# Delta rule on a hybrid diffusion step: triangular solves in blocks of 16 instead of 32, a convolution that accumulates in PSUM, and transfers issued on GpSimd and ACT

## The chip, the cores and the metric

One core of a Trainium2 chip runs the whole program. The metric is the device time of one execution in microseconds, taken over several executions; a separate profiled execution gives the trace. The core's engines are called by their names in the profile: PE is TensorE (matrix products, with PEld for its weight loads), DVE is VectorE, ACT is ScalarE, POOL is GpSimd and SP is SyncE, which here does nothing but issue transfers. Each engine takes its instructions in order, from a list that is fixed when the program is built.

## The reference, cut to what matters

The program is one step of a two-layer model over 640 tokens (128 of a prompt and 512 of a sample) of width 1024. Layer 0 mixes tokens with a state-space scan and attention, layer 1 with a gated delta rule; each layer ends in a two-matrix MLP with a hidden width of 4096. The change lies mostly in the delta rule of layer 1, which the reference computes as follows (for both directions of time, 8 heads of 128 channels, chunks of 64 tokens there):

```python
proj = h @ w_in
qkv = silu(dwconv(proj[..., :3 * D_MODEL], conv_w))       # 5 taps along the tokens
g = -exp(a_log) * softplus(a_in + dt_bias)                # log decay, per head
beta = sigmoid(b_in)
q, k = l2norm(q) * DN_DK ** -0.5, l2norm(k)
# in _gdn_chunked, per chunk
decay  = exp(where(tri_incl, gcum[..., :, None] - gcum[..., None, :], -inf))
a_mat  = where(tri_strict, (kb @ k.T) * decay, 0.0)       # the Gram block
t_mat  = triangular_solve(eye + a_mat, eye)               # the solve
u_c, w_c = t_mat @ (v * beta), t_mat @ (kb * exp(gcum))
# a scan over chunks with the state s
v_new = u_i - w_i @ s
o     = (q_i * exp(g_i)) @ s + at_i @ v_new
s     = s * exp(g_last) + (k_i * exp(g_last - g_i)).T @ v_new
# after the scan
out = (rmsnorm(o_f + o_b) * silu(z)) @ w_out
```

## The kernel before, in words

The kernel keeps the 640 tokens along the free dimension and channels on the partitions. A list planner of the framework orders the instructions of every engine when the program is built: each instruction has a priority from its place in the program, a block under `high_priority(offset=n)` counts as if it stood n instructions earlier, and a buffer (a tile with a tag and a number of `bufs`) is handed on when its last reader is done. PSUM is divided into four tags of two banks each, `pg`, `pa`, `pb` and `pc`.

**Matrix products of projections and MLPs.** `gemm` walks over blocks of 128 output channels. `weight` loads one block of weights (512 KB, tile `raw`, two buffers) with a transfer issued on SP, ACT rounds it to a high part `whi` (L194) and POOL subtracts to get the low part `wlo` (L196). `mm_step` then makes three products per 128 input channels, in two halves of 320 tokens: L205, L206 and L207, 48 matrix products for a block. This routine serves 153 weight blocks of the whole program.

**Layer 1** (the method `odd`) works on four pairs of heads, `pr` 0 to 3. `gdn_project` makes the pair's six blocks of k, q and v (`m` 0 to 5). Its `ev` evacuates each block to the SBUF tile `cb` with padding columns, and runs the convolution there: an ACT multiplication for tap 0 (L1319), four DVE multiply-adds over 642 columns (L1322), an ACT tanh, and a last DVE multiply-add in two pieces (L1335, L1336). For some blocks the last tap or the last product is made by ACT and POOL instead (L1325 and L1326; L1331 to L1333). Squares, transposes to token order and normalization follow, with banks of tag `pc`.

**Gram blocks.** `gdn_group` is called once for each of five chunks of 128 tokens, out of `mid`. It makes the decay matrix (POOL L1376, ACT L1379), the Gram product in a `pb` bank (PE L1395), the products with decay (DVE L1400) and beta (POOL L1401), and writes the result to DRAM (`udg`, `utd`), from where the 32x32 diagonal blocks return to the tile `ub`, one block in each of 80 partitions.

**The solve.** `gdn_blocks` inverts these 32x32 triangles by elimination: 31 steps of two DVE instructions each, a product into `sbt` (L1425) and a subtraction from `ub` (L1427), on 31 to 256 elements. `gdn_inverse` then builds the 128x128 inverses: ten POOL products with a mask and ten DVE transposes for a pair (twice: L1453, L1454), and 140 small matrix products in `pb` banks (L1458), first to 64x64 and then to 128x128.

**The chain.** `gdn_chain` runs the scan over the chunks: `prep` loads what a step needs (`cka`, `ckb`, `cbc`, `cgq`), multiplies q by its decay on POOL (four products, L1567) and makes the attention block (PE L1570); then come PE L1615, L1625, L1631, L1632 and L1643 with DVE L1620 and L1646 between them. Chains 0 to 2 use banks `pa`, the last one `pb`.

**Order.** `solve` calls what is left of the pair's `blocks` generator (that is `gdn_blocks`), then `gdn_inverse` and `gdn_chain` at an offset of 10000. In the program it stands behind the projection of the next pair. For the last pair, the eight blocks of the gate z (`zproj`, evacuation L1721 to L1724) are put in, too. Behind all that stand filling products of the modulation (L282), the gating, and the output projection in two halves (`odd` and `odd_out`, residual in L423).

Transfers: all of them are issued on SP, one after the other.

## Time and profile before

| what | value |
|---|---|
| time, median of 3 runs | 1972.41 us (1968.0 to 1977.28) |
| time of the profiled execution | 1975.42 us |
| its span, first to last instruction | 1973.2 us |
| mean granted TensorE clock | 0.965 |
| PE busy | 1798.4 us (91%) |
| DVE busy | 1279.3 us (65%) |
| ACT busy | 875.5 us (44%) |
| POOL busy | 760.1 us (39%) |
| transfers | 286.60 MB, 45.4% of 16 engines' time on the SP queue |

The profile lists, for the profiled execution, when each instruction ran, on which engine and for how long, which instruction ended an engine's wait, and which clock TensorE was granted. A matrix product of 32-bit operands that are not rounded appears in it as two records. "Busy" of a group is the time in which at least one of its instructions ran.

### The profile page before, as it was taken

What the parts mean: (1) busy time and instruction counts of PE and PEld (TensorE: products, weight loads), DVE (VectorE), ACT (ScalarE), POOL (GpSimd) and SP (SyncE); (2) the same over time, 40 slices, a digit from 0 to 9 for tenths busy, and PEclk for the clock granted to TensorE, in tenths of its full rate; (3) what the DMA queues carried; (4) which work ended last, traced back from release to release, by engine and by line L of the source; (5) the groups of instructions that cost most, each with busy time, mean ns of one, the idle gap of its engine ahead of it and who ended that gap; (6) DMA issues with size and microseconds to landing.
All of it is one profiled execution on the core that took longest, in us unless ns stands there. A gap on an engine that the chain in (4) does not pass through costs nothing. (4 is left out here: it accounts for less than half of the span.)

```text
span 1973.2 us, 35750 instructions
## 1 busy us (share of the span) xinstructions
PE 1798.4 (91%) x13556; PEld 1696.1 (86%) x13556; DVE 1279.3 (65%) x2797; ACT 875.5 (44%) x1956; POOL 760.1 (39%) x609
## 2 busy tenths in 40 slices
PE   5789799989999999997878888798989899999998
PEld 3789677978999999997877888787878799999997
DVE  8998777269273644547589988674667927364553
ACT  4344466344243443535454455344324425344362
POOL 2522101541343343453455555522245334343451
PEclk9989899999999999998998999999999999999999
DMA  8446886533332222332576468758844122222221
GB/s 319 131 122 167 248 264 205 201 121 126 109 117 76 77 85 82 135 117 72 163 208 197 117 196 239 222 166 269 274 137 149 54 97 76 86 76 86 76 97 54
DMA packets 206983, 286.60 MB, mean 145 GB/s; under 512 B 54878, under 2 KB 138236, under 8 KB 206812
## 3 DMA queue, kind: packets, MB, share of 16 engines
q1 hardware_dynamic: 206812, 284.33, 45.4%
q8 instruction: 107, 1.75, 0.4%
q14 instruction: 64, 0.52, 0.1%
HBM read 228.87 MB, written 46.82 MB: 140 GB/s over the span
## 5 line engine op out<-in xcount | busy, mean ns | idle before, releaser
L196 POOL TENSOR_TENSOR wlo<-raw,whi 128x1024 fp32r<-128x1024 f32 (+1 forms) x153 | 359.3, 2351 | 509.1 <-ACT whi L194 462.3
L194 ACT ACTIVATE whi<-raw 128x1024 fp32r<-128x1024 f32 (+1 forms) x153 | 153.1, 1001 | 329.1 <-PE pg L206 146.8
L207 PE MATMUL pg<-hidh,wlo 128*128 128x320 f32 (+2 forms) x576 | 178.8, 311 | 0.6 <-POOL wlo L196 0.6
L205 PE MATMUL pg<-hidh,whi 128*128 128x320 f32 (+2 forms) x576 | 179.0, 311 | 0.0
L206 PE MATMUL pg<-hidl,whi 128*128 128x320 f32 (+2 forms) x576 | 178.9, 311 | 0.0
L423 DVE SCALAR_TENSOR_TENSOR x<-pg,mod,x 128x128 f32<-128x128 f32 (+2 forms) x132 | 53.7, 436 | 182.2 <-PE pg L207 182.2
L205 PE MATMUL pg<-h10h,whi 128*128 128x320 f32 x472 | 158.4, 336 | 14.7 <-DVE cb L1722 7.0
L207 PE MATMUL pg<-h10h,wlo 128*128 128x320 f32 x472 | 155.4, 329 | 1.7 <-POOL wlo L196 1.7
L206 PE MATMUL pg<-h10l,whi 128*128 128x320 f32 x472 | 155.7, 330 | 0.0
L205 PE MATMUL pa<-hidh,whi 128*128 128x320 f32 x448 | 138.0, 310 | 1.1 <-ACT whi L194 1.1
L207 PE MATMUL pa<-hidh,wlo 128*128 128x320 f32 x448 | 138.4, 309 | 0.0
L206 PE MATMUL pa<-hidl,whi 128*128 128x320 f32 x448 | 138.2, 309 | 0.0
L423 DVE SCALAR_TENSOR_TENSOR x<-pa,mod,x 128x128 f32<-128x128 f32 (+2 forms) x108 | 43.9, 435 | 133.1 <-PE pa L207 133.1
L508 POOL TENSOR_TENSOR wq<-S,wq 128x512 fp32r<-128x512 f32 x52 | 71.3, 1371 | 115.3 <-ACT wq L507 115.3
L205 PEld LDWEIGHTS pg<-h10h,whi 128*128 128x128 f32 x472 | 95.8, 203 | 18.3 <-DVE cb L1722 8.0
L207 PEld LDWEIGHTS pg<-hidh,wlo 128*128 128x128 f32 x576 | 108.2, 188 | 1.6 <-POOL wlo L196 1.1
L205 PEld LDWEIGHTS pg<-hidh,whi 128*128 128x128 f32 x576 | 108.3, 188 | 0.9 <-issue 0.8
L206 PEld LDWEIGHTS pg<-hidl,whi 128*128 128x128 f32 x576 | 108.2, 188 | 0.4 <-DVE hidl L569 0.3
L1322 DVE SCALAR_TENSOR_TENSOR cv<-cb,cw,cv 128x642 f32<-128x642 f32 x90 | 95.8, 1065 | 10.4 <-ACT cv L1319 9.2
L207 PEld LDWEIGHTS pg<-h10h,wlo 128*128 128x128 f32 x472 | 95.4, 202 | 2.1 <-POOL wlo L196 1.9
L206 PEld LDWEIGHTS pg<-h10l,whi 128*128 128x128 f32 x472 | 95.7, 203 | 0.6 <-issue 0.4
L205 PEld LDWEIGHTS pa<-hidh,whi 128*128 128x128 f32 x448 | 83.9, 188 | 2.7 <-ACT whi L194 1.8
(743 smaller groups left out, 5745.4 us busy)
## 6 DMA issues: line engine op xcount, KB each, us to landing
raw<-in_wff SPq DMA_DIRECT2D x104, 512.0 KB
mraw<-in_wmod SPq DMA_DIRECT2D x96, 512.0 KB
raw<-in_wino SPq DMA_DIRECT2D x33, 512.0 KB
rawx<-in_wff SPq DMA_DIRECT2D x24, 512.0 KB
raw<-in_wine SPq DMA_DIRECT2D x16, 512.0 KB
cka<-pd SPq DMA_DIRECT2D x28, 256.0 KB
ckb<-pd SPq DMA_DIRECT2D x28, 256.0 KB
s5g<-s5g SPq DMA_DIRECT2D x32, 164.0 KB
```

The lines of the kernel that those rows point to most:

```text
L194: nc.scalar.activation(hi[:, :kt], raw[:, :kt], AF.Copy)
L196: (nc.vector if self.lov and self.nw % self.lov else nc.gpsimd).tensor_tensor(lo[:, :kt], raw[:, :kt], hi[:, :kt], op=ALU.subtract)
L205: nc.tensor.matmul(p[:, :n], hi[:, k], xh[:, s], start=(k == 0), stop=False)
L206: nc.tensor.matmul(p[:, :n], hi[:, k], xl[:, s], start=False, stop=False)
L207: nc.tensor.matmul(p[:, :n], lo[:, k], xh[:, s], start=False, stop=(k == kt - 1))
L423: nc.vector.scalar_tensor_tensor(x[m][:, s], p[:, ls], g, x[m][:, s], op0=ALU.mult, op1=ALU.add)
L508: (V if j % 2 else nc.gpsimd).tensor_tensor(t[:, 4:8], src, t[:, 0:4], op=SU)
L1322: V.scalar_tensor_tensor(cv, cb[m][:, t:t + 642], cw[:, t:t + 1], cv, op0=M, op1=AD)
```

## The change

1. `gdn_blocks` inverts 16x16 triangles: the two halves of each 32x32 block at once, 15 steps of two DVE instructions on 30 to 128 elements, into a tile of its own (`ubd`, set to zero by POOL). `ub` has one buffer instead of two.
2. `gdn_inverse` gets a first stage that joins 16x16 inverses into 32x32 ones: 160 matrix products of 32x32x32 for a pair, two ACT copies, two DVE subtractions. The mask products on POOL and most transposes go; ACT copies place the blocks. The other 140 products now name a row of the array as well as a column. Its loads from DRAM go from 3 to 14 transfers, issued on SP.
3. The convolution (`conv`) works on the prompt's 128 columns in SBUF and on the sample's 512 columns in a PSUM bank of tag `pc`, all taps and the last product on DVE, for all 24 blocks.
4. Gram products use `pc` banks instead of `pb`. `solve` is called when `m == 1` of the next pair's projection has been evacuated, in front of that pair's Gram blocks; `gdn_blocks` is called at the end of its own pair's projection.
5. Issue of transfers: all weight loads of `weight` and the store `udg` move from SP to GpSimd, the stores `ed` and `zod` to ACT.
6. The product of q with its decay moves from POOL (four instructions of 128 columns) to DVE (two of 256). The evacuation of z uses another buffer.

```diff
@@ weight
-        nc.sync.dma_start(out=raw[:, :kt], in_=src)
+        nc.gpsimd.dma_start(out=raw[:, :kt], in_=src)
@@ gdn_project
+        def conv(x, cw):
+            cv = self.tl([128, 642], "cv")
+            cl = self.ps("pc")
+            parts = ((cv[:, 0:128], 0), (cl, 130))
+            for o, c0 in parts:
+                nc.scalar.activation(o, x[:, c0:c0 + o.shape[1]], AF.Identity, scale=cw[:, 0:1])
+            for t in range(1, 5):
+                for o, c0 in parts[::-1]:
+                    V.scalar_tensor_tensor(o, x[:, c0 + t:c0 + t + o.shape[1]], cw[:, t:t + 1], o, op0=M, op1=AD)
+            for o, c0 in parts[::-1]:
+                nc.scalar.activation(x[:, c0:c0 + o.shape[1]], o, AF.Tanh)
+            for (o, c0), c1 in zip(parts[::-1], (128, 0)):
+                V.scalar_tensor_tensor(cv[:, c1:c1 + o.shape[1]], x[:, c0:c0 + o.shape[1]], 1.0, o, op0=AD, op1=M)
+            return cv
@@ gdn_group
-        nc.sync.dma_start(out=ed[:, c], in_=E)
-        pk = self.ps("pb")
+        nc.scalar.dma_start(out=ed[:, c], in_=E)
+        pk = self.ps("pc")
...
-            nc.sync.dma_start(out=self.ap(ud, o + 10 * d * self.US, [[128, 128], [self.US, 2], [1, 128]]),
+            nc.gpsimd.dma_start(out=self.ap(ud, o + 10 * d * self.US, [[128, 128], [self.US, 2], [1, 128]]),
@@ gdn_blocks
-        D = ub
-        V.memset(D.rearrange("p a b -> p (a b)")[:, 0:1024:33], 1.0)
-        for j in range(31):
-            n, m = 31 - j, j + 1
...
+        D = P.tile([80, 32, 32], F32, name="ubd", bufs=1)
+        nc.gpsimd.memset(D, 0.0)
+        nc.gpsimd.memset(D.rearrange("p a b -> p (a b)")[:, 0:1024:33], 1.0)
+        for j in range(15):
+            n, m = 15 - j, j + 1
+            sh = [80, 2, n, m]
...
+            V.tensor_tensor(t, both(ub, j, 1, j + 1, n).rearrange("p s a b -> p s b a").to_broadcast(sh),
+                            both(D, j, 1, 0, m).to_broadcast(sh), op=ALU.mult)
+            V.tensor_tensor(both(D, j + 1, n, 0, m), both(D, j + 1, n, 0, m), t, op=ALU.subtract)
@@ gdn_inverse
-        cm = P.tile([128, 20, 32], F32, name="gcm")
-        nc.sync.dma_start(out=cm, in_=self.ap(dd, 0, [[32, 128], [4096, 20], [1, 32]]))
+        Dc, Tc, Gc, Xc = (P.tile([128, 2, 10, 32], F32, name=n) for n in ("gDc", "gTc", "gGc", "gXc"))
+        for d, t in ((0, Dc), (1, Tc)):
+            for hh in range(2):
+                nc.sync.dma_start(out=t[:, d, hh::2], in_=...)
+        G.memset(Gc, 0.0)
+        for d in range(2):
+            for k in range(4):
+                nc.sync.dma_start(out=Gc[r:r + 16, d, :, j:j + 16], in_=...)
-        for c in range(5):
-            for d, a, b in ((0, D, TT), (1, TT, D)):
-                G.tensor_tensor(a[...], src, mask, op=ALU.mult)
-                V.transpose(two(b, c, d), two(a, c, d))
+        V.transpose(fl(Tc[:, 0]), fl(Dc[:, 0]))
+        V.transpose(fl(Dc[:, 1]), fl(Tc[:, 1]))
+        px = [bank() for d in range(2)]
+        for d in range(2):
+            for n in range(10):
+                for r in S:
+                    mm(px[d][r, n], Gc[r, d, n], Dc[r, d, n], r.start, r.start)
+            ACT.activation(Xc[:, d], px[d], AF.Copy)
+        px = [bank() for d in range(2)]
+        for d in range(2):
+            for n in range(10):
+                for r in S:
+                    mm(px[d][r, n], Tc[r, d, n], Xc[r, d, n], r.start, r.start)
+            V.tensor_tensor(Dc[:, d], Dc[:, d], px[d], op=ALU.subtract)
+            V.transpose(fl(Tc[:, d]), fl(Dc[:, d]))
+        G.memset(D64, 0.0)
+        G.memset(TT, 0.0)
...
@@ gdn_chain, prep
-                for u in range(4):
-                    nc.gpsimd.tensor_tensor(gq[:, u], gq[:, u], lds[u][2 + u % 2], op=M)
+                for d in range(2):
+                    V.tensor_tensor(gq[:, 2 * d:2 * d + 2], gq[:, 2 * d:2 * d + 2], lds[2 * d][8], op=M)
@@ odd
-            th = self.tl([128, HB], "cb")
+            th = self.sp.tile([128, HB], F32, name="zth", tag="acc", bufs=2)
...
-            nc.sync.dma_start(out=zds[m][:, s], in_=th)
+            nc.scalar.dma_start(out=zds[m][:, s], in_=th)
...
             def mid(m, pd):
+                if m == 1 and held:
+                    solve(*held)
...
+                if m == 5:
+                    got.append(next(steps[0]))
             pd = self.gdn_project(pr, hn, P, first if pr == 0 else None, mid)
-            if held:
-                solve(*held)
-            held = pr, pd, steps[0]
+            held = pr, pd, got[0]
```

## Rows read from the trace of the kernel before

**Rows 1.** The page's list of engines: busy us, share of the span, instructions.
```profile
PE 1798.4 (91%) x13556; PEld 1696.1 (86%) x13556; DVE 1279.3 (65%) x2797; ACT 875.5 (44%) x1956; POOL 760.1 (39%) x609
```
**Rows 2.** Stretches: length, busy PE, PEld, DVE, ACT, POOL, granted clock, transfers.
```profile
600.00:700.00 100.00, 100.00 (x684) 100.00 (x684) 48.39 (x90) 39.49 (x76) 40.20 (x23) 1.00 0.25 80
880.00:1020.00 140.00, 119.28 (x784) 114.47 (x783) 99.34 (x187) 78.33 (x171) 63.08 (x78) 0.91 0.49 143
1020.00:1160.00 140.00, 114.00 (x964) 109.94 (x963) 136.86 (x263) 70.12 (x149) 80.67 (x75) 0.89 0.54 158
1160.00:1330.00 170.00, 148.56 (x1499) 139.08 (x1498) 131.36 (x352) 81.90 (x195) 82.60 (x89) 0.96 0.74 211
1330.00:1465.00 135.00, 122.29 (x1173) 106.86 (x1171) 68.51 (x214) 47.86 (x112) 34.52 (x50) 0.97 0.73 239
```
**Rows 3.** A stretch of L1425 alone: DVE busy, mostly the elimination of pair 0.
```profile
1020.00:1100.00 80.00, 18.20 (x34) 0.89 0.56 168
```
**Rows 4.** Stretches of L1458 alone (PE, PEld): the inverse of pair 0.
```profile
990.00:1100.00 110.00, 0.00 (x0) 0.00 (x0) 0.89 0.64 186
1100.00:1140.00 40.00, 6.21 (x280) 5.13 (x280) 0.91 0.44 121
```
**Rows 5.** Layer 1 as one stretch: DVE time of L1425, L1427, L1322, in this order.
```profile
880.00:1465.00 585.00, 64.70 (x124) 0.94 0.63 189
880.00:1465.00 585.00, 72.58 (x124) 0.94 0.63 189
880.00:1465.00 585.00, 95.76 (x90) 0.94 0.63 189
```
**Rows 6.** DVE's timeline: start us, us, instruction; then POOL's.
```profile
1030.31 0.27 DVE L1427 TENSOR_TENSOR ub<-ub,sbt 80x112 f32<-80x112 f32 x1
1030.61 0.29 DVE L1425 TENSOR_TENSOR sbt<-ub 80x135 f32<-80x135 f32 x1
...
1052.23 2.49 DVE L1427 TENSOR_TENSOR ub<-ub,sbt 80x252 f32<-80x252 f32 x1
...
1051.88 2.57 POOL L196 TENSOR_TENSOR wlo<-raw,whi 128x1024 fp32r<-128x1024 f32 x1
```
**Rows 7.** Single lines of DVE: shortest, median and longest in ns.
```profile
L1400 DVE TENSOR_TENSOR gau<-pb,gbg x20: 674/678/692, 972.2 to 1253.0; 128x512 f32<-128x512 f32 x20
L1322 DVE SCALAR_TENSOR_TENSOR cv<-cb,cw,cv x90: 758/878/3014, 909.6 to 1246.8; 128x642 f32<-128x642 f32 x90
L1335 DVE SCALAR_TENSOR_TENSOR cv<-cb,cv x16: 277/280/427, 922.6 to 1256.6; 128x128 f32<-128x128 f32 x16
```
**Rows 8.** POOL by line and shape, 840 to 1500: busy us, mean ns.
```profile
L1567 POOL TENSOR_TENSOR cgq<-cgq,cka 128x128 f32<-128x128 f32 x64 | 31.8, 524 | 84.6 <-DVE cgl L1565 45.4 <-DMA cka<-pd 22.5 <-DVE ogn_t L180 7.7
...
L1453 POOL TENSOR_TENSOR gTT<-gcm,cst 128x256 f32<-128x256 f32 x20 | 18.6, 932 | 0.0
...
L1453 POOL TENSOR_TENSOR gD<-gcm,cst 128x256 f32<-128x256 f32 x20 | 16.2, 811 | 11.8 <-DMA gcm<-dd 11.8
L1333 POOL TENSOR_TENSOR cv<-cb,cv 128x512 f32<-128x512 f32 x8 | 12.0, 1502 | 0.0
L1326 POOL TENSOR_TENSOR cv<-cv,cb 128x642 f32<-128x642 f32 x6 | 9.9, 1646 | 5.9 <-ACT cb L1325 5.9
```
**Rows 9.** PE by line and shape, 840 to 1500: small products of the inverse.
```profile
L1458 PE MATMUL pb<-gD,guf 128*32 128x32 f32 x320 | 8.3, 210 | 10.9 <-DVE gD L1454 6.7 <-DVE osm L1663 3.7 <-POOL gD L1453 0.3
...
L1458 PE MATMUL pb<-gTT,gcm 128*32 128x32 f32 x320 | 4.8, 199 | 0.0
```
**Rows 10.** SP's own waits, 880 to 1470: us in total, times, longest.
```profile
SPq L193 <- POOL wlo L196: 46.0, 13, 7.3
SPq L1724 <- ACT cb L1723: 26.0, 6, 11.4
```
**Rows 11.** SP issuing weight loads (shortest, median, longest ns).
```profile
L193 SPq DMA_DIRECT2D raw<-in_wino x33: 327/376/1099, 855.5 to 1293.6; - x33
```
**Rows 12.** The page's groups: POOL's share of preparing all weight blocks.
```profile
L196 POOL TENSOR_TENSOR wlo<-raw,whi 128x1024 fp32r<-128x1024 f32 (+1 forms) x153 | 359.3, 2351 | 509.1 <-ACT whi L194 462.3
```

More of the change, by code (lines that the diff above doesn't have):

```diff
@@ L1455, in gdn_inverse @@
-        CH = [(c, hh) for c in range(5) for hh in range(2)]
-        def mm(out, l, r, col):
-            nc.tensor.matmul(out, l, r, start=True, stop=True, tile_position=(0, col))
-        def bank(n):
-            return self.ps("pb")[:, :320].rearrange("p (c h j) -> p c h j", c=5, h=2)
-        p = bank(0)
-        for c, hh in CH:
+        D64 = P.tile([128, 10, 64], F32, name="gD64")
+        fl = lambda t: t.rearrange("p n j -> p (n j)")
+        V.transpose(fl(Tc[:, 0]), fl(Dc[:, 0]))
+        V.transpose(fl(Dc[:, 1]), fl(Tc[:, 1]))
@@ new lines, in mm, with bank @@
+        def mm(out, l, r, row, col):
+            nc.tensor.matmul(out, l, r, start=True, stop=True, tile_position=(row, col))
+        def bank():
+            return self.ps("pb")[:, :320].rearrange("p (n j) -> p n j", n=10)
+        S = [slice(32 * k, 32 * k + 32) for k in range(4)]
+        px = [bank() for d in range(2)]
[4 more added lines that the diff above has]
+            ACT.activation(Xc[:, d], px[d], AF.Copy)
@@ L1466, in gdn_inverse @@
+        for d in range(2):
+            for r in S:
+                ACT.activation(TT[r, :, u2(d), r], ch(Tc[r, d]), AF.Copy)
+            for k in range(2):
+                r = S[2 * d + k]
+                ACT.activation(D64[r, :, 32 * k:32 * k + 32], Dc[r, d], AF.Copy)
+        p = bank()
+        for n in range(10):
+            c, hh = divmod(n, 2)
             for a in (0, 64):
                 x, y = slice(a, a + 32), slice(a + 32, a + 64)
-                mm(p[y, c, hh], uo[:, 0, c, hh, a:a + 32], D[:, c, hh, x], a + 32)
@@ L1476, in gdn_inverse @@
-        ACT.activation(D[32:64, :, 0:2, 0:32], pD[32:64], AF.Copy, scale=-1.0)
-        ACT.activation(D[64:96, :, 2:4, 96:128], pD[64:96], AF.Copy, scale=-1.0)
-        for c, hh in CH:
+        pD, pT = bank(), bank()
+        for n in range(10):
+            mm(pD[32:64, n], Tc[32:64, 0, n], X[32:64, n], 32, 32)
+            mm(pD[64:96, n], Tc[64:96, 1, n], X[64:96, n], 64, 64)
+        ACT.activation(D64[32:64, :, 0:32], pD[32:64], AF.Copy, scale=-1.0)
+        ACT.activation(D64[64:96, :, 32:64], pD[64:96], AF.Copy, scale=-1.0)
@@ L1479, in gdn_inverse @@
+        for n in range(10):
             for a in (0, 64):
                 x, y = slice(a, a + 32), slice(a + 32, a + 64)
[L1481 to L1482 removed]
+                mm(pT[x, n], X[y, n], Tc[y, 0, n], a + 32, a)
+                mm(pT[y, n], X[x, n], Tc[x, 1, n], a, a + 32)
         for a in (0, 64):
             x, y = slice(a, a + 32), slice(a + 32, a + 64)
[L1485 removed]
@@ new lines, in gdn_inverse @@
+        parts = ((0, 8), (8, 10))
+        for n0, n1 in parts:
+            p = self.ps("pb").rearrange("p (n j) -> p n j", n=8)
+            for n in range(n0, n1):
+                c, hh = divmod(n, 2)
+                mm(p[y, n - n0], uo[x, 0, c, hh, 32:96], D64[x, n], 0, 64)
+                mm(p[x, n - n0], uo[y, 1, c, hh, 0:64], D64[y, n], 64, 0)
+            ACT.activation(Y[:, n0:n1], p[:, :n1 - n0], AF.Copy)
+        for n0, n1 in parts:
+            p = self.ps("pb").rearrange("p (n j) -> p n j", n=8)
+            for n in range(n0, n1):
+                c, hh = divmod(n, 2)
+                mm(p[x, n - n0], Y[y, n], TT[y, c, hh, y], 64, 0)
+                mm(p[y, n - n0], Y[x, n], TT[x, c, 2 + hh, x], 0, 64)
+            ACT.activation(TT[x, n0 // 2:n1 // 2, 0:2, y], ch(p[x, :n1 - n0]), AF.Copy, scale=-1.0)
+            ACT.activation(TT[y, n0 // 2:n1 // 2, 2:4, x], ch(p[y, :n1 - n0]), AF.Copy, scale=-1.0)
@@ L1542, in load @@
                     nc.sync.dma_start(out=a[k], in_=pd["pd"][:, c, 4 * k:4 * k + 4])
-                held[c] = [a[k][:, i] for k in range(2) for i in range(4)]
+                held[c] = [a[k][:, i] for k in range(2) for i in range(4)] + [a[0][:, 2:4]]
             return held[c]
@@ L1741, in rest, with solve @@
             ods.append(self.gdn_chain(pr, pd, TT, P, *((self.LATE, "pb") if late else (self.CHAIN, "pa"))))
-        def solve(pr, pd, steps):
-            *_, g = steps
+        def solve(pr, pd, g):
             with tc.high_priority(offset=10000):
@@ L1773, in odd @@
             nc.sync.dma_start(out=x[k], in_=xd[k])
-        zt = P.tile([128, 4, T], F32, name="gD")
+        zt = [P.tile([128, T], F32, name=n) for n in ("gTc", "gGc", "gXc", "gD64")]
         ot = P.tile([128, 3, T], F32, name="guf")
```

91 lines of the change are left out of this document (27 added, 64 removed).

## The prediction

> **What bounds the kernel now.** I read the page's list of engines first: PE is busy 91% of the span, DVE 65% [rows 1]. So the kernel as a whole hangs on PE, and the question is where PE is not fed. The stretches say it: in an MLP (600 to 700 us) PE is busy all the time at full clock, 684 products in 100 us, which is 7.0 us for the 48 products of one weight block. In layer 1 (880 to 1465) it is not. Its four pieces have 20.7, 26.0, 21.4 and 12.7 us without PE work, and a granted clock of 0.91, 0.89, 0.96 and 0.97; 1.00 is the level of 2.4 GHz and the pieces mix it with the lower one [rows 2]. Counting the share below 1.00 as lost over the whole piece (too much, since part of it falls into idle time) adds 12.6, 15.4, 6.8 and 4.0 us. So PE loses at most 33, 41, 28 and 17 us there, 119 in all. This is all that the change can win back in its own layer; everything else of the kernel changes only in who issues the weight loads.
>
> Why PE waits: from 1020 to 1160 DVE is busy 136.9 of 140 us, PE 114.0 [rows 2]. DVE is the bound of that piece. Next view, what DVE does: the elimination L1425 and L1427 takes 64.7 + 72.6 = 137.3 us of the 436.1 that the four pieces have, the convolution's taps L1322 95.8 us [rows 5, 2]. The elimination of pair 0 is the better part of the 34 products that lie between 1020 and 1100, threaded between convolutions [rows 3], and no product of an inverse runs before 1100 [rows 4]: inverse and chain of a pair come one projection late because the elimination is late.
>
> Then the timeline: a step of the elimination on 112 or 135 elements takes 0.27 or 0.29 us, but one on 252 takes 2.49 us, beside a POOL subtraction of 2.57 us that began 0.35 us earlier [rows 6]. DVE instructions with both operands in SBUF wait for a POOL instruction to end; L1322 ranges from 758 to 3014 ns. L1400, with one operand in PSUM, stays between 674 and 692 over 20 instructions [rows 7].
>
> **The change part by part.**
>
> *Elimination.* Before, 248 instructions of 31 to 256 elements. After, 120 of 30 to 128 elements, 1360 elements on each side of a pair's 30. From 0.27 us at 112 and 0.29 at 135 elements [rows 6] I take 0.15 us + 1 ns per element: 15 steps of two come to 2 x (15 x 0.15 + 1.36) = 7.2 us a pair, 29 in all. Waits for POOL can stretch that: the old ones would cost 2 x (31 x 0.15 + 5.46) = 20.2 us a pair or 81 us by the same rule and took 137, a factor of 1.7. So 29 to 49 us, and I take 39: DVE gives up 98 us. The two POOL memsets in front of it hide behind the Gram transfers that it waits for anyway.
>
> *Convolution.* Before, 90 taps L1322 (95.8 us) and 16 ends of 0.68 + 0.28; the price of L1336 is that of L1400, the same 512 columns. After, 24 times five pairs of 512 and 128 columns at 0.68 and 0.28 us [rows 7]: 115 against 96 + 15 = 111 us. DVE pays 4 us, and 82 of the 115 can no longer be stopped by POOL.
>
> *Decay of q.* 32 DVE products of 256 columns, between 0.28 us (128) and 0.76 (642) [rows 7], so 0.40 each: 13 us. POOL drops 31.8 us [rows 8]. Transposes fall from 40 to 16, eight subtractions come: nought.
>
> DVE in all: -98 + 4 + 13 = -81 us of 436, which leaves 355 in 585 us (61%). DVE stops being a bound; what is late next is PE.
>
> *New products of the inverse.* 160 a pair, 640 in all, 1280 records. The trace has no 32-row products. The nearest ones, with 128 rows and 32 columns, come at 8.3 us / 320 = 26 ns and 4.8 / 320 = 15 ns a record [rows 9]; the first group holds waits between them. That bounds them by 19 and 33 us, and I take 19, since the new ones are issued in uninterrupted runs of 40, as the second group is. They are work that PE did not have. The Trainium skill, TensorEngine Tiling (Array Packing), Key Properties, says that tiles in different places of the array load and multiply at the same time; by it four of them would run together, the price would be about 5 us, and the sum 14 us lower. No row here shows products that name rows as well as columns.
>
> *POOL.* It drops the masks (18.6 + 16.2), the convolution's part (12.0 + 9.9 and a smaller group) and the decay of q (31.8), at least 88 us [rows 8] of 260.9 [rows 2]. It gains memsets and the issue of transfers: in layer 1 33 blocks for the projections, 8 of the output projection and 40 `udg`, 81 in all. The trace has no transfer issued on POOL. From below, SP needs 0.33 us [rows 11]; from above, I take a whole subtraction of a block, 2.4 us [rows 12]. 27 to 194 us; nearer to the lower end, 1 us each, 81. POOL then stands where it stood, hidden: a load waits only for POOL's own subtraction and an ACT rounding that this subtraction waited for already, and nothing new stands behind it. In the MLPs a block has 7.0 us, POOL needs 2.4 for it; the issue is free there up to 4.6 us.
>
> *SP and ACT.* SP loses the waits for POOL in front of weight loads (46.0 us) and for ACT in front of `zod` (26.0) in layer 1 [rows 10], behind which the chain's loads stood. It gains 11 transfers a pair, 44 x 0.38 = 17 us [rows 11]. I count neither: 0, with up to 10 us of gain where ACT and POOL waited for chain loads. ACT issues 36 stores (some 12 us at SP's price) and copies blocks; it is busy 278 of 585 us [rows 2].
>
> *The place of the solve.* Its priority puts it ahead of the projection already, so the call's place by itself counts nothing. That the elimination is short, and Gram products no longer share `pb` with the inverse, brings inverse and chain forward.
>
> *The sum.* Of the piece that DVE bounds (41 us) I take back 80%, 33; DVE there falls from 137 to some 90 us. Of 1160 to 1330 (28 us, DVE 77% busy) half, 14. Of the two others (50 us) a fifth, 10. That is 57. Minus 19 for the new products, minus 2 for waits on the convolution's bank: -36 us. The profiled execution took 1975.4 us (span 1973.2 and 2.2 around it), so 1939; it lies 3.0 above the median of the three runs, 1972.4, and against that the forecast is **1936 us**, within 1915 and 1958 if this is how it goes (30 to 80 us won back, products at 15 to 26 ns). From no change one can tell about 0.5%, 10 us.
>
> **The rivals.**
>
> *The chains come forward as a whole.* The tail behind the last projection shrinks as well: nine tenths of 41, three quarters of 28 and half of 50 are 83 us, less 19: 1908. For it: every chain waited for an elimination. Against: the last piece has PE busy 122 of 135 us.
>
> *PE takes the place of DVE.* Only the 33 us of the DVE-bound piece come back and the products cost 33: 1972. For it: PE is at 87 to 91% in the other late pieces, and work is added to it.
>
> *The convolution holds a bank (the slow one).* One of the two `pc` banks is taken from ACT's first tap to the end, at least 0.68 + 4 x 0.96 + 0.68 + 0.68 = 5.9 us (ACT's two passes taken at DVE's 0.68 [rows 7]), 24 times. The other serves 64 uses: per pair two squares, six transposes to tokens, three of keys, five Gram products. PE stands in order, so each that finds no bank stops everything behind it. If this leaves 38 us won, it decides from 38 / 64 = 0.6 us of waiting per use; at 1 us, 26 us are lost: 1998. For it: the convolution needed no bank before, and Gram products come to `pc`, too. Against: 24 x 5.9 and 64 uses at 2 us, an estimate of three times L1400, are 270 us of the 600 and more that two banks offer in 300.
>
> *Weight loads come late from POOL.* It decides where issue plus subtraction pass the 7.0 us of a block, at 4.6 us of issue. At 5.5 us the blocks of the MLPs loaded this way (6 + 4 x 8 in each of two layers) lose 0.9 us each, 68 us, against the gain of 36: 2004. For it: no row shows the price. Against: SP's own issues of the projections' loads take 1.1 us at most [rows 11]. The Trainium skill, SBUF — State Buffer, two separate sides (the box on DVE blocking DMA), speaks against this part: a GpSimd transfer waits for its descriptors while DVE holds the ports that both share, 3.1 us instead of 0.62 in its example. By that the wait is below the 4.6 us, so it would cost nothing in the MLPs; no run here shows it.
>
> **How the numbers follow.** The forecast gets 0.48, the larger gain 0.12, PE in DVE's place 0.18, the bank 0.13, late loads 0.09. Faster by over 0.5% (below 1962): 0.48 + 0.12 + 0.04 of the third, about 0.63, after a little for the forecast's edge. Slower (above 1982): 0.13 + 0.09 = 0.22. Within: 0.15. The range is 1905 to 1990: it holds the forecast and PE in DVE's place, most of the larger gain and the mild half of the slow ones.
>
> **What would show it.** In the new profile: L1425's and L1427's successors at 30 to 50 us together; taps on PSUM at 0.68 us with no spread; the first product of an inverse some 60 us earlier than 1100; DVE near 60% in layer 1; granted clock near 1.00 between 1020 and 1160; the small products at 15 to 26 ns a record. Wrong would be: PE waiting for `pc` banks with DVE's convolution as the one that frees them, PE waiting for `whi` or `wlo` in the MLPs, or a PE that is as idle as before with DVE idle, too.

## The result and the profile after

The changed kernel takes 2077.0 us (2074.0 to 2078.8, 4 runs) against 1973.7 (4 runs): a ratio of 1.0525 with a 95% interval of 1.0496 to 1.0554, **103 us slower** where 36 us faster was forecast.

The page of the changed kernel: its engines' busy time, then PE's busy share and its granted clock, in tenths, in 40 slices of 51.9 us (busy times before: [rows 1]):

```profile
span 2077.0 us, 38336 instructions
PE 1844.7 (89%) x14836; PEld 1737.7 (84%) x14836; DVE 1245.1 (60%) x2799; ACT 899.7 (43%) x2046; POOL 779.1 (38%) x696
PE   5898899989999999978769997892798799999998
PEclk9899999989999999988779898896798899999999
```

The clock of the kernel before, in 40 slices of 49.3 us, nowhere lies below 8 tenths:

```profile
PEclk9989899999999999998998999999999999999999
```

PE is busy 46 us longer, DVE 34 us less, and the span grew by 104 us. The clock says where: four slices lie at 6 or 7 tenths, from 987 to 1090 and from 1402 to 1506 us, and in these PE was busy 7, 6, 2 and 7 tenths of the time. The MLPs are out of it (600 to 700: 684 products, PE busy 100 us, as in [rows 2]).

So I cut layer 1 at the first product of the projections, the last of the z projection, and the last of the output projection, and call the two stretches the projections and the tail. First the kernel before, then the changed one (from:to length, then busy PE, PEld, DVE, ACT, POOL, the granted clock, DMA share, GB/s):

```profile
882.30:1360.70 478.40, 404.18 (x3576) 384.03 (x3572) 376.10 (x829) 241.33 (x538) 234.52 (x253) 0.92 0.60 175
1360.70:1504.20 143.50, 130.82 (x1023) 116.75 (x1022) 81.83 (x233) 47.56 (x108) 51.37 (x58) 0.98 0.67 226
```

```profile
887.00:1412.70 525.70, 444.66 (x4453) 423.73 (x4453) 333.07 (x829) 261.87 (x625) 201.38 (x242) 0.87 0.53 155
1412.70:1601.40 188.70, 128.54 (x1400) 111.32 (x1398) 82.69 (x231) 52.00 (x114) 50.04 (x50) 0.78 0.58 184
```

The projections lost 47 us, the tail behind them 45, what lies ahead 5, what follows 7. DVE was relieved (457.9 to 415.8 us) and PE did not gain: its idle time in the two stretches rose from 86.9 to 141.2 us, 60 of them in the tail, where it had 13. In the projections most of the loss is busy time: PE was busy 40 us longer there and idle 7 us longer. What PE waited for from 880 to 1620 (us in all, times, longest):

```profile
PE pc L282 <- DMA mraw<-in_wmod: 39.2, 4, 33.1
PE pb L1463 <- DMA gDc<-dd: 16.2, 6, 10.6
PE pc L1272 <- ACT tsq L1268: 15.0, 4, 6.7
```

One wait of 33.1 us, for a modulation row. The timeline around it (start, length, engine, line; idle before, and what ended it):

```profile
1412.86 0.82 PE L1299 MATMUL pc<-cst,cv 128*128 128x128 f32 x6
1414.94 0.71 PE L1394 MATMUL pc<-khT 128*128 128x128 f32 x4
...
1428.41 3.81 SPq L1449 DMA_DIRECT2D gGc<-udg  x8
...
1435.77 0.37 SPq L1411 DMA_DIRECT2D ub<-udg  x1
...
1440.88 0.19 DVE L1428 TENSOR_TENSOR sbt<-ub,ubd 80x30 f32<-80x30 f32 x1 [9.02 <-DMA ub<-utd]
...
1449.18 0.37 SPq L269 DMA_DIRECT2D mraw<-in_wmod  x1
1449.66 0.37 SPq L1432 DMA_DIRECT2D dd<-ubd  x1
1453.58 1.08 PE L282 MATMUL pc<-mraw,scond 128*32 128x256 f32 x8 [33.15 <-DMA mraw<-in_wmod]
```

The last pair's fifth Gram group (L1394) runs at 1414.9, behind the transposes of the values (L1299) and the whole z projection, which has a higher priority than those; in the kernel before it was at 1239. Its elimination starts at 1440.9, after its loads (L1411) stood on SP behind the eight new `gGc` loads and others from 1428.4 to 1435.8. Only when the elimination lets go of `ub` does the modulation row start (L269), behind which PE stands: from 1413.6 to 1453.6 it was busy 2.5 of 40 us, and the granted clock of these 40 us was 0.56. All 80 records of the Gram products in the kernel before, in the kernel before with the Gram products in `pc` (an experiment below) and in the changed one (shortest, median, longest ns; first and last start):

```profile
L1395 PE MATMUL pb<-khT x80: 270/275/581, 971.0 to 1238.9; 128*128 128x128 f32 x80
L1395 PE MATMUL pc<-khT x80: 270/275/582, 968.6 to 1319.7; 128*128 128x128 f32 x80
L1394 PE MATMUL pc<-khT x80: 271/276/583, 964.4 to 1415.4; 128*128 128x128 f32 x80
```

### The profile page after: what moved, and what is told of

The parts are those of the page before. It is cut to its first block, busy times and chain, and to the rows that moved or that the text cites. A ratio compares the mean times of both kernels' runs of the same rounds, so it can differ in the third digit from the quotient of the medians.

```text
span 2077.0 us, 38336 instructions
## 1 busy us (share of the span) xinstructions
PE 1844.7 (89%) x14836; PEld 1737.7 (84%) x14836; DVE 1245.1 (60%) x2799; ACT 899.7 (43%) x2046; POOL 779.1 (38%) x696
## 4 chain that ended last, share of the span: by engine, by line
PE 61%; DVE 18%; DMA 11%; issue 4%; ACT 3%; POOL 1%; SPq 1%; POOLq 0%; ACTq 0%; DVEq 0%
PE pg L206 7%; PE pg L205 7%; PE pg L207 7%; PE pa L206 4%; PE pa L207 4%; PE pa L205 4%; DMA mraw<-in_wmod 2%; PE pg L526 2%; PE pg L528 2%; PE pg L527 2%; PE pb L526 2%; PE pb L528 2%; PE pa L526 2%; PE pa L528 2%; PE pa L527 2%
## 5 line engine op out<-in xcount | busy, mean ns | idle before, releaser
L196 POOL TENSOR_TENSOR wlo<-raw,whi 128x1024 fp32r<-128x1024 f32 (+1 forms) x153 | 351.9, 2302 | 647.0 <-ACT whi L194 602.8
L205 PE MATMUL pg<-hidh,whi 128*128 128x320 f32 (+2 forms) x576 | 179.4, 311 | 0.0
L207 PE MATMUL pg<-hidh,wlo 128*128 128x320 f32 (+2 forms) x576 | 179.0, 311 | 0.2 <-POOL wlo L196 0.2
L205 PE MATMUL pg<-h10h,whi 128*128 128x320 f32 x472 | 159.5, 338 | 1.5 <-DVE zth L1753 0.7
L207 PE MATMUL pg<-h10h,wlo 128*128 128x320 f32 x472 | 156.0, 330 | 0.0
L205 PE MATMUL pa<-hidh,whi 128*128 128x320 f32 x448 | 138.6, 311 | 1.7 <-ACT whi L194 1.7
L207 PE MATMUL pa<-hidh,wlo 128*128 128x320 f32 x448 | 138.6, 310 | 0.0
L207 PEld LDWEIGHTS pg<-hidh,wlo 128*128 128x128 f32 x576 | 108.4, 188 | 1.0 <-POOL wlo L196 0.4
L205 PEld LDWEIGHTS pg<-hidh,whi 128*128 128x128 f32 x576 | 108.4, 188 | 0.9 <-PE pc L282 0.4
L205 PEld LDWEIGHTS pg<-h10h,whi 128*128 128x128 f32 x472 | 97.2, 206 | 3.0 <-ACT cb L1331 1.1
L207 PEld LDWEIGHTS pg<-h10h,wlo 128*128 128x128 f32 x472 | 96.5, 204 | 0.2
L282 PE MATMUL pc<-mraw,scond 128*32 128x256 f32 x448 | 41.3, 423 | 57.5 <-DMA mraw<-in_wmod 55.6
L205 PEld LDWEIGHTS pa<-hidh,whi 128*128 128x128 f32 x448 | 84.0, 188 | 3.6 <-ACT whi L194 2.0
```

Source lines behind the costliest of these rows:

```text
L196: (nc.vector if self.lov and self.nw % self.lov else nc.gpsimd).tensor_tensor(lo[:, :kt], raw[:, :kt], hi[:, :kt], op=ALU.subtract)
L205: nc.tensor.matmul(p[:, :n], hi[:, k], xh[:, s], start=(k == 0), stop=False)
L207: nc.tensor.matmul(p[:, :n], lo[:, k], xh[:, s], start=False, stop=(k == kt - 1))
L282: nc.tensor.matmul(p[32 * i:32 * i + 32, :256], self.sc[:, 4 * kh + i], raw[:, i], start=(kh == 0), stop=(kh == 1), tile_position=(0, 32 * i))
```

## The experiments

Theories at the start: A, the order on PE at the end of the layer; B, the new inverse costs more than it saves; C, weights from POOL come late; D, the convolution holds the bank. Each was measured against the kernel before on the same chip; behind a time stands its ratio to that kernel with the 95% interval.

### The new inverse by itself

From the kernel before: `gdn_blocks` and `gdn_inverse` of the change, with one `ub` beside `ubd`; everything else as before.

> The kernel before with one part of the change alone: the elimination on blocks of 16 and the new inverse with its 32-row products (and, because they need the memory, one buffer `ub` beside `ubd`, and the modulation rows in these two). Weights, convolution, Gram bank, q's decay, stores and the place of the solve are those of before. Theory A (the order on PE is at fault: in the changed kernel the last pair's fifth Gram group stands behind the whole z projection, at 1415 us, the last elimination ends at 1449, and the modulation products behind it wait 33 us for rows that need `ub` and `ubd`): here the last pair's Gram products and inverse stand ahead of the last third of the z projection, so that stall is gone and the last chain runs beside the modulation products: 1940 to 1975 us, no wait of over 5 us for a modulation row. Theory B (the new inverse itself costs more than it saves: 1280 more products, a lower granted clock): 2010 to 2080 us. Theory C (weights issued on POOL come late): below 2000 us too, since they are issued on SP here; it is told from A by the run with weights on SP.

Measured: 1997.2 us, 1.0110 (1.0087 to 1.0132). Its two stretches:

```profile
883.40:1412.40 529.00, 451.47 (x5132) 428.08 (x5129) 334.29 (x747) 281.79 (x638) 215.40 (x249) 0.92 0.61 175
1412.40:1528.80 116.40, 105.84 (x748) 91.29 (x746) 59.65 (x174) 31.27 (x65) 45.63 (x43) 0.93 0.62 207
```

Between A and B. The tail shrinks by 27 us, as the chains come earlier (the last inverse starts at 1312 in place of 1338); the projections lengthen by 51, and part of that is work that stood in the tail before (PE's busy time in the tail falls from 130.8 to 105.8 us). PE's idle time in the two stretches is 88.1 us, as before, with 64 us less busy time of DVE; PE was busy 22 us longer, so the loss is busy time.

### The elimination cut, without new products

```diff
-        for j in range(31):
-            n, m = 31 - j, j + 1
+        for j in range(15):
+            n, m = 15 - j, j + 1
```

The elimination's other steps and elements are left out, and nothing takes their place.

> The kernel before with the elimination cut to its first 15 steps on at most 64 elements; the rest of each block's elimination is left out, and nothing takes its place. VectorE drops about 100 us of work and TensorE has none of the new products. Theory A (the prediction's: VectorE bounds a part of the layer, 57 us come back where it is relieved): 1905 to 1930 us, TensorE's idle time in the layer falls from 87 to some 35 us. Theory B (TensorE's idle time there doesn't hang on VectorE; in the run with the new inverse alone it was 88 us with 64 us less work on VectorE): 1965 to 1985 us, idle time 75 to 95 us. Between them: what it gains is the worth of the relief, and the 22 us that the new inverse alone lost, plus this, are the price of the new products and their waits.

Measured: 1951.1 us, 0.9894 (0.9868 to 0.9920).

```profile
880.80:1364.00 483.20, 415.57 (x3773) 396.91 (x3770) 334.53 (x748) 254.63 (x578) 228.12 (x267) 0.93 0.65 189
1364.00:1484.40 120.40, 111.32 (x826) 98.38 (x825) 63.10 (x193) 33.94 (x70) 47.58 (x46) 0.96 0.62 207
```

The relief of DVE is worth 20 us, not 57: idle time of PE falls from 86.9 to 76.7 us only. The two lines of the elimination take 44.7 us in place of 137.3; DVE's busy time in the two stretches falls by 60, since other work of DVE, the convolution's among it, runs longer. The piece from 1020 to 1160, where DVE was busy 136.9 us and PE idle 26.0 [rows 2], says it most clearly. With the elimination cut, and then in the changed kernel:

```profile
1020.00:1160.00 140.00, 116.24 (x1190) 109.98 (x1191) 112.41 (x224) 72.03 (x167) 82.09 (x94) 0.89 0.68 189
1020.00:1160.00 140.00, 114.03 (x1302) 109.82 (x1303) 103.09 (x262) 74.60 (x187) 54.48 (x73) 0.87 0.62 174
```

DVE is busy 112 and 103 us, and PE is still idle 23.8 and 26.0. The longest of PE's waits in this piece, again with the elimination cut and then in the changed kernel (us in all, times, longest):

```profile
PE pb L1458 <- DVE gD L1454: 9.8, 8, 4.5
PE pb L1463 <- DMA gDc<-dd: 10.6, 1, 10.6
```

In the kernel before the first product of an inverse ran at 1108, and PE's longest waits in the piece were for a convolution (6.3 us) and for a step of the chain (4.2). Now the inverse comes earlier in this piece, and its own waits, for its transposes on DVE or for its loads from DRAM, take the place of those that went.

### Each new product twice

```diff
-                    mm(px[d][r, n], Gc[r, d, n], Dc[r, d, n], r.start, r.start)
+                    for _ in range(2):
+                        mm(px[d][r, n], Gc[r, d, n], Dc[r, d, n], r.start, r.start)
```

and the same for the second round, in the kernel with the new inverse alone.

> The kernel before with the new inverse alone, and each of its 1280 new 32-row products (both rounds, all pairs) issued twice into the same place; loads, copies and waits around them stay. The plan's order is nearly that of the new inverse alone. Theory P (the products' own time on TensorE is what costs): 22.8 us of busy time more, so 1997 plus 15 to 30: 2012 to 2027 us. Theory W (the loads, copies and waits of the two added rounds cost, the products run into TensorE's idle time): within 8 us of the new inverse alone, 1990 to 2005 us. If products in different places of the array ran wholly side by side, as a page's rule has it (the Trainium skill, TensorEngine Tiling (Array Packing), Key Properties), the second set would add some 5 us: under 2005 us too, told from W by the busy time of the products themselves.

Measured: 2029.7 us, 1.0272 (1.0250 to 1.0294): 32 more, above even theory P. The products of the two rounds in the single and in the doubled kernel (count of records, two to a product; busy us, mean ns of one record, idle before):

```profile
L1481 PE MATMUL pb<-gDc,gGc 32*32 32x32 f32 x640 | 9.6, 198 | 3.6 <-issue 1.9 <-DVE gau L1417 1.7
L1481 PE MATMUL pb<-gXc,gTc 32*32 32x32 f32 x640 | 8.3, 200 | 3.1 <-issue 2.4 <-DVE gau L1417 0.8
```

```profile
L1481 PE MATMUL pb<-gXc,gTc 32*32 32x32 f32 x1280 | 22.2, 225 | 7.9 <-issue 4.7 <-DVE gau L1417 3.2
L1481 PE MATMUL pb<-gDc,gGc 32*32 32x32 f32 x1280 | 18.1, 210 | 16.1 <-issue 11.4 <-ACT gXc L1494 2.8 <-DVE gau L1417 1.0
```

17.9 us became 40.3, and the waits in front of them 6.7 became 24.0. So a set of products costs some 30 us. Less the 20 that the short elimination gives, that is 10 to 12 of the 22 that the new inverse loses; about 10 stay open. Two more rounds of loads and copies could be one reason, and the trace shows another: in the kernel with the new inverse alone the 1968 large products L205 to L207 of the two stretches, the same in number, were busy 6 us longer than before, at a granted clock of 0.93 in place of 0.98 in the tail.

### Weights issued on POOL

On the kernel before, `nc.sync` becomes `nc.gpsimd` in the load of `raw`; and the reverse on the changed kernel.

> The kernel before with the weight loads issued on POOL, nothing else. From the changed kernel with its weights on SP, which took 17 us less: if this price stands by itself, 1988 to 1996 us, with the loss at the seams (the start of the last MLP, the first projections) and none where TensorE is busy all the time; if it belongs only to the changed kernel's order of work, 1970 to 1980 us; if loads from POOL come late in the MLPs' steady part too, above 2000 us and under 684 products in 100 us there.

> The changed kernel with the weight loads issued on SP as before, nothing else altered. Theory C (weights on POOL come late): 1975 to 2010 us. Theory A: the last pair's Gram group stays behind the whole z projection and the wait for the modulation row stays at 25 us or more: 2060 to 2085 us. In the MLPs no difference by either reading of the profile, where PE is busy all the time with loads issued on POOL (100 of 100 us between 600 and 700).

Measured: 2000.8 us, 1.0147 (1.0130 to 1.0165) on the kernel before; 2060.4, 1.0434 (1.0414 to 1.0455) on the changed one, 17 less than it. The loss lies ahead of layer 1 (7 us), in the projections (11) and in the tail (8), not in the steady part of an MLP (684 products in 100 us from 600 to 700, as before). Loads and subtractions of some blocks in the projections, in the kernel before and with POOL as the issuer (L1332 and L1333 are the convolution's part on POOL):

```profile
1076.29 2.51 POOL L196 TENSOR_TENSOR wlo<-raw,whi 128x1024 fp32r<-128x1024 f32 x1
1079.70 0.35 SPq L193 DMA_DIRECT2D raw<-in_wino  x1
1089.80 2.45 POOL L196 TENSOR_TENSOR wlo<-raw,whi 128x1024 fp32r<-128x1024 f32 x1
1092.28 0.34 SPq L193 DMA_DIRECT2D raw<-in_wino  x1
```

```profile
1082.46 2.60 POOL L196 TENSOR_TENSOR wlo<-raw,whi 128x1024 fp32r<-128x1024 f32 x1 [1.68 <-ACT whi L194]
...
1089.57 0.59 POOL L193 DMA_DIRECT2D raw<-in_wino  x1
...
1094.45 2.60 POOL L196 TENSOR_TENSOR wlo<-raw,whi 128x1024 fp32r<-128x1024 f32 x1 [3.41 <-DVE ub L1427]
...
1098.94 0.59 POOL L193 DMA_DIRECT2D raw<-in_wino  x1
...
1102.03 2.49 POOL L196 TENSOR_TENSOR wlo<-raw,whi 128x1024 fp32r<-128x1024 f32 x1 [2.32 <-ACT whi L194]
1109.66 0.95 POOL L1332 TENSOR_TENSOR cv<-cb,cv 128x128 f32<-128x128 f32 x1 [5.13 <-ACT cb L1331]
1110.58 4.70 POOL L1333 TENSOR_TENSOR cv<-cb,cv 128x512 f32<-128x512 f32 x1
1115.23 0.59 POOL L193 DMA_DIRECT2D raw<-in_wino  x1
```

SP issues 0.9 and 0.0 us after the subtraction that frees the buffer, POOL 4.5, 1.9 and 10.7 us after it: on POOL the load stands in order behind other work, in the last case behind a product that waited 5.1 us for ACT and one that took 4.7. The issue itself is 0.59 us. That the line on POOL makes the 30 us is read from these rows; whether a transfer issued on POOL also takes longer to land was not tried (the page gives a median of 5.0 us for the projections' loads on POOL and none for those on SP).

### The other parts alone

Each on the kernel before: stores of the decay and of z on ACT and `udg` on POOL; `pk = self.ps("pc")`; the new `conv`; q's decay on DVE.

> The kernel before with the stores of the decay and of the z projection issued on ACT and `udg` on POOL, as in the changed kernel, nothing else. The prediction counted 0 with up to 10 us of gain, since SP waited 26.0 us for ACT and elsewhere for POOL in front of chain loads: 1962 to 1980 us. If POOL's issue (0.74 us each, measured, 40 of them) held up its subtractions for the weights: 1980 to 1995 us.

> The kernel before with the Gram products in `pc` in place of `pb`, nothing else. On TensorE the last fifth group moves from block 26 to 28.5 and the last inverse from 32 behind the z projection, among the modulation products. Theory A2: the last chain ends later by up to the length of those 4 blocks, 10 to 25 us: 1980 to 1995 us. If only the joint hold with the convolution costs: 1965 to 1978 us.

> The kernel before with the new convolution (512 columns in a `pc` bank, none of it on POOL), nothing else. The prediction counted plus 4 us of VectorE and some 2 us of waits on the bank, so within 10 us: 1965 to 1985 us. If the bank is short even without Gram products in it (64 - 20 uses): 1990 to 2010 us. The trace of the changed kernel has the taps at 142 us together where the prediction had 115, so VectorE pays about 30 us; by the worth of its relief (20 us for 105 us of work) that is 6 us.

> The kernel before with the decay of q on VectorE (32 products of 256 columns in place of 64 on POOL), nothing else. The prediction counted plus 13 us on VectorE and minus 31.8 us on POOL, and nothing on TensorE: 1965 to 1980 us. By the worth of VectorE's relief found since (20 us for 105), 13 us cost 2 to 3; if the plan's order is what each part disturbs, as with the stores and the Gram bank: 1985 to 1995 us.

Measured: stores 1988.3 us, 1.0094 (1.0072 to 1.0116); Gram in `pc` 1993.3, 1.0107 (1.0076 to 1.0139); convolution 1972.3, 0.9997 (0.9980 to 1.0013); q 1970.8, 0.9968 (0.9953 to 0.9983). With the Gram products in `pc` alone the last fifth group already slips from 1239 to 1319 us. Which of the three stores costs the 18 us was not tried. The call of the solve at its old place, with all else as changed, gives the same instructions in the same order on all five engines as at its new one, so in the changed kernel it costs nothing; with the Gram products in `pb` the order differs, as the next section shows.

### The end of the layer

Five kernels change what the last pair meets, all from the changed kernel: the Gram groups written ahead of the values' transposes,

```diff
-            if m == 5:
-                tok(2)
             if mid:
                 mid(m, pd)
+            if m == 5:
+                tok(2)
```

the Gram products in `pb` with the solve's call as before, the same with the call as changed, the convolution of before, and the modulation rows in `raw` in place of `ub` and `ubd`.

> The changed kernel with two statements swapped: at the last projection of a pair the Gram groups are written ahead of the transposes of the values, so that the fifth group asks for its `pc` bank first. Banks, convolution, issue of transfers and all amounts of work are as changed; on TensorE the last pair's fifth Gram group now stands at block 26 of 33, its inverse at 30.5 to 31.4. Theory A2 (the fifth Gram group stands in the line for `pc` behind transposes that the planner puts behind the whole z projection): the stretch from the end of the z projection to the end of the output projection falls from 189 to some 120 us, the time to 2000 to 2020 us, and no wait of over 10 us for a modulation row is left. Theory D (the convolution's hold of the bank itself): above 2055 us, since it holds it as long as before.

> The changed kernel with the Gram products in `pb` as before and the solve called behind the projection as before; all else as changed, the convolution's bank too. Theory A (order on PE, because Gram products and the transposes of values share `pc` with the convolution): the last pair's Gram products stand at 26 of the 33 blocks, its inverse between blocks 27 and 29, so its elimination ends before 1330 us, the 33 us wait for a modulation row goes and the tail behind the z projection shortens by some 65 us: 2000 to 2030 us. Theory B (new inverse is the cost): 2060 to 2080 us. Theory C (weights on POOL): 2060 to 2080 us. Theory D (the convolution's own hold of a `pc` bank is the cost): at most 20 us better than the changed kernel, 2055 to 2077 us.

> The changed kernel with the Gram products alone back in `pb`; the solve's call stays ahead of the next groups. On TensorE the last pair's fifth Gram group stands behind the whole z projection here too. Theory A2 (the place in the order, not the bank): 2050 to 2080 us, the last stretch 170 us or more. If the shared bank by itself were the cost: 2015 to 2035 us, as with the solve's place changed too.

> The changed kernel with the convolution of before (taps on 642 columns in SBUF, a part on POOL, no PSUM bank). Theory A: the last Gram group comes at 28.5 of the 33 blocks in place of 33, the inverse just before the end of the z projection; the stall on the modulation row shrinks from 33 to under 15 us: 2015 to 2050 us. Theory D (the bank that the convolution holds is what costs): 1960 to 2000 us, and the waits for squares and transposes in `pc` fall from 15.0 and 6 us to under 10 together. Theories B and C: 2060 to 2085 us, since neither the inverse nor the issue of weights is altered.

> The changed kernel with the modulation rows in the two buffers `raw` of the weights in place of `ub` and `ubd`; nothing else. The order on TensorE is the same up to the end of the z projection; then 48 modulation products stand ahead of the last inverse. Theory A1 (the wait of 33 us for a row that needs `ub` and `ubd` is itself the cost): 2040 to 2050 us. Theory A2 (the last pair's late Gram group is the cost, and the wait only shows where TensorE has nothing else): 48 products of 0.38 us, on four columns' places at a time some 5 us, move into the gap, and the last elimination still ends near 1449 us: 2062 to 2080 us.

Measured against before: 2019.9 us, 1.0230 (1.0195 to 1.0265); 2022.6, 1.0237 (1.0215 to 1.0259); 2051.7, 1.0406 (1.0361 to 1.0450); 2018.1, 1.0210 (1.0179 to 1.0242); 2070.1, 1.0514 (1.0468 to 1.0560). The swap of two statements alone gives back 57 of 103 us, with the convolution, the bank and every amount of work as changed (lines: the projections and the tail):

```profile
887.30:1424.00 536.70, 448.43 (x5088) 427.43 (x5087) 350.57 (x897) 277.31 (x666) 202.91 (x245) 0.89 0.58 167
1424.00:1548.90 124.90, 108.27 (x770) 95.40 (x772) 62.02 (x164) 33.97 (x74) 48.28 (x47) 0.89 0.64 215
```

Of these 57 us, 38 are idle time of PE and 18 its busy time (page: 1844.7 to 1826.5 us), though no product is left out: the same products took less time, at a granted clock of 0.89 in both stretches in place of 0.87 and 0.78.

The bank by itself is not the cost either. Back in `pb`, with the call of the solve as changed, 25 us return, and the fifth Gram group stands behind the whole z projection as before (1395); with the call as before it comes at 1306, and 54 return. So with the Gram products in `pb` the place of the call is worth 29 us.

The modulation row was not the cost: without its wait for `ub` the ratio falls from 1.0525 to 1.0514, nothing clear of noise, and the last inverse still starts at 1454. Theory D falls too. The convolution of before undoes the delay, but so does the swap, which leaves the convolution alone. Across eleven of the kernels the tail follows, roughly, how long before the end of the z projection the last inverse starts (from the timelines, us; the one with the convolution of before lies off):

| kernel | fifth Gram group | last inverse starts | z projection ends | tail |
|---|---|---|---|---|
| new inverse alone | 1235 | 1312 | 1412 | 116 |
| Gram in `pb`, solve as before | 1306 | 1357 | 1427 | 120 |
| swap | 1325 | 1377 | 1424 | 125 |
| before, new convolution | 1264 | 1344 | 1378 | 124 |
| before | 1239 | 1338 | 1361 | 144 |
| before, weights on POOL | 1260 | 1358 | 1379 | 151 |
| changed, convolution of before | 1343 | 1393 | 1411 | 128 |
| before, q on DVE | 1238 | 1341 | 1338 | 155 |
| before, Gram in `pc` | 1320 | 1398 | 1373 | 158 |
| changed, Gram in `pb` | 1395 | 1438 | 1395 | 183 |
| changed | 1415 | 1457 | 1413 | 189 |

A short tail is not yet a fast kernel: with q on DVE the tail is 155 us, and yet it is among the fastest, since its projections end 23 us earlier.

### A better kernel?

The z projection below the modulation products in priority (on the kernel before); q's decay with the new convolution; q's decay with that priority.

> The kernel before with the z projection's priority put below that of the modulation products; no work is changed. The modulation products now stand between the last inverses, and the z projection lasts until the last chain. In the runs so far the stretch behind the z projection was 116 to 120 us where the chains came early and 143 in the kernel before. If the order of work is what is left to win: 1950 to 1965 us. If TensorE's idle time only moves from one stretch to the other: 1967 to 1980 us. If the modulation rows' loads, for which there are two buffers that the elimination shares, stop TensorE in the middle: 1985 us or more.

> The kernel before with the two parts of the change that alone lost nothing: the convolution in a `pc` bank and the decay of q on VectorE. If both stand by themselves: 1962 to 1972 us. If VectorE, which takes some 60 us more by the two, becomes the bound in the first projections: 1978 to 1990 us.

> The kernel before with the decay of q on VectorE and the z projection's priority below that of the modulation products. If the two add up: 1962 to 1972 us. If the order of the z projection only moves idle time: as with q's decay alone, 1968 to 1973 us.

Measured: 1974.5 us, 0.9989 (0.9975 to 1.0002); 1991.8, 1.0086 (1.0066 to 1.0107); 1974.9, 1.0002 (0.9988 to 1.0016). Nothing beyond q's 0.3%, and that is gone with the z projection moved as well. Two parts that cost 0 and -6 us alone cost 17 together: the planner lays out the layer anew for each edit, and prices of parts don't add.

## Why the prediction was wrong

**The elimination, q, the products: right.** In the changed kernel (lines of DVE, POOL and PE in the layer; busy us, mean ns):

```profile
L1428 DVE TENSOR_TENSOR sbt<-ub,ubd 80x30 f32<-80x30 f32 (+7 forms) x60 | 20.6, 344 | 21.1 <-DMA ub<-utd 16.1 <-DMA ub<-udg 3.9
L1430 DVE TENSOR_TENSOR ubd<-ubd,sbt 80x30 f32<-80x30 f32 (+7 forms) x60 | 19.1, 318 | 1.1
L1598 DVE TENSOR_TENSOR cgq<-cgq,cka 128x256 f32<-128x256 f32 x32 | 13.4, 432 | 9.9 <-DMA cka<-pd 9.8
L1318 DVE SCALAR_TENSOR_TENSOR pc<-cb,cw,pc 128x512 f32<-128x512 f32 x96 | 70.7, 746 | 14.6 <-ACT pc L1315 13.9
L1318 DVE SCALAR_TENSOR_TENSOR cv<-cb,cw,cv 128x128 f32<-128x128 f32 x96 | 47.9, 499 | 12.0 <-ACT cv L1315 9.9
L1403 POOL DMA_DIRECT2D udg<-gau x40 | 29.4, 737 | 3.9 <-POOL gau L1400 3.3 <-issue 0.3 <-POOL cb L1329 0.3
L193 POOL DMA_DIRECT2D raw<-in_wino x31 | 17.8, 575 | 5.5 <-POOL wlo L196 5.1 <-PE pa L1646 0.3
L1463 PE MATMUL pb<-gDc,gGc 32*32 32x32 f32 x640 | 12.8, 223 | 16.7 <-DMA gDc<-dd 16.2 <-DVE gDc L1460 0.5
L1463 PE MATMUL pb<-gXc,gTc 32*32 32x32 f32 x640 | 10.0, 224 | 5.0 <-issue 5.0
```

Elimination 39.7 us (39 was taken, the middle of 29 to 49), q 13.4 (13), products 22.8 in busy time (19; bounds 19 and 33). Issue on POOL 0.57 and 0.74 us (1). The call of the solve at its new place: nothing in the changed kernel, as counted, though 29 us with the Gram products in `pb`; that its priority alone settles the place did not hold there.

**The convolution: mis-sized, without effect on the time alone.** Taps and ends took 142 us in place of 115 (the ends 23.7 of them): a tap on the 128 columns in SBUF took 0.50 us on average (median 0.35, longest 3.81) where 0.28 was taken, one on the 512 in PSUM 0.75 (longest 0.76) where 0.68 was. Alone it cost 0, but in the change it took back part of DVE's relief: 42 us less busy time in the two stretches, where 81 were forecast for the layer.

**First failed step: "Of the piece that DVE bounds (41 us) I take back 80%, 33", and the 57 of the sum.** The cut elimination shows 20. DVE was busy 98% there [rows 2], but that it was busy beside an idle PE did not make it the bound: with DVE at 112 of 140 us PE's idle time in that piece falls from 26.0 to 23.8 us, and in the two stretches 77 of 87 us remain. The inverse that comes earlier brought waits of its own, 9.8 and 10.6 us, which the sum put at nothing. One sign that the prediction named for being wrong is what came: a PE as idle as before with DVE idle, too. With products that cost some 30 us by the doubling, where 19 were taken, the new inverse loses where the sum had a gain. The rival in which relief and products cancel (1972 us) had this part of the mechanism.

**Second: "Gram products no longer share `pb` with the inverse, brings inverse and chain forward".** For the first pair the inverse did come forward: its first product runs at 1062 in place of 1108 us, 46 earlier where some 60 were forecast, and at 1055 where only the elimination is cut and the Gram products stay in `pb`. For the last pair it was the reverse: in `pc` its fifth Gram group stands in line with the values' transposes, and the last inverse starts at 1457 in place of 1338. The swap, which changes this order alone, makes the tail 64 us shorter and the kernel 57 us faster. The bank's rival (1998 us) had the place, `pc`, but not the mechanism: the swapped kernel holds the bank for the convolution as long, and the convolution alone costs 0. The price lies in the order that is laid out around the banks.

**Third: POOL, "nothing new stands behind it", and 0 for SP and ACT.** Right in the MLPs, as argued. In the layer's in-order POOL queue a load stood up to 10.7 us behind its buffer's release. Issuing on POOL costs 30 us alone and 17 in the changed kernel. The rival of late loads had the sign, but at the wrong place (the MLPs, by a slow issue). Moving the stores cost 18 where 0 to 10 us of gain stood.

**The range.** The inner bounds of 1915 to 1958 do not follow from their terms either: 30 us won back, less 33 for the products and 2 for the bank, is some 1977.

So of the 103 us, 57 are shown to be the last pair's order and 17 the weights on POOL, each by one edit of the changed kernel. The new inverse costs 22 on the kernel before, which is near what is left; that the three add up is not shown, since other parts, alone, did not add. By place it is 47 in the projections, 45 in the tail and 11 ahead of and behind them.

## What to carry to other kernels

Relieve a busy engine in a trial that leaves its work out before paying another engine for the relief: DVE was 98% busy beside an idle PE, and 60 us less of its busy time gave 20 us. When operations move to another bank or queue, ask who stands in that line at the end of the stage, where nothing is left to fill a wait; a move that is free in a steady MLP costs in a mixed stage. With a planner between code and chip, parts don't add: test the order alone.

## What was not expected of the hardware

A record of a 32-row product takes 198 to 225 ns, but by the groups' busy time one ends every 13 to 20 ns; the products of the kernel before, over all 128 rows, did so every 15 to 26 ns [rows 9]. The Trainium skill, TensorEngine Tiling (Array Packing), Key Properties, has tiles in different places working at the same time. By the estimate that I drew from it 1280 records would cost 5 us, and they took 17.9 to 22.8, so the fourfold gain of that estimate did not show. All four places of a round write into one PSUM bank here (`px[d]` in the diff), and no run gives them banks of their own, so the reason stays open. In long runs of them PE also paused for nothing that the profile shows ("issue"): 4.3 us, and 16.1 when doubled.

POOL issued a weight transfer in 0.53 to 0.97 us with DVE busy 90% of the time beside it (layer 0, weights on POOL alone). The Trainium skill, SBUF — State Buffer, two separate sides (the box on DVE blocking DMA), has 3.1 us in its example; no row here shows that. By the rows shown, the loads came late by the line on POOL and not by the issue.
